# Residual rows added by accumulating loads, transposes and operand sums moved by a product, three operand fetches and one weight sum moved behind the last residual

## The chip, the cores and the metric

The kernel runs on one core of a Trainium2 chip, as one program. The metric is the device time of that program in microseconds. The core has a matrix engine (PE, with its weight loads shown as PEld), a vector engine (DVE), an activation engine (ACT), a general engine (POOL) that also issues DMAs, and a sync engine (SP) that only issues DMAs. Each engine takes its own instructions in the order that the build gave them, and waits on semaphores for the others. Sixteen DMA engines move all data.

## The reference

One layer of a hybrid decoder, on one sequence of 512 tokens with a model width of 2048, all in float32:

```python
h = rmsnorm(x, g_mix)
z = h @ w_in                         # conv B, C, V | attn Q, K, V | forget logits | two gates
...
merged = gc * conv_branch + ga * attn_branch
x = x + merged @ w_mix_out           # the mixing: this change
h = rmsnorm(x, g_mlp)
u = square(relu(h @ w_ff1))          # the MLP; its first group is fed by the mixing
x = x + u @ w_ff2
return rmsnorm(x, g_final)
```

The change concerns the line with `w_mix_out` and the hand-over to `w_ff1`.

## The kernel before

**Products.** Every large matrix product is done as a 2 by 2 block scheme with seven products in place of eight, named A11, A12, S1, S2, S3, S4 and A22. Each block operand is split into a high part and a low part (`split`, L102: the high part by a copy on ACT at L103, the low part by a subtraction on DVE at L104), and each product runs high by high, low by high and high by low, 48 matmuls for the blocks here. A class `Group` (from L190) does one set of 512 output columns: it loads the four quarters of the weights (`load`, on SP), splits them one after another into a pair of buffers of which there are two, runs the products into PSUM banks a, b, c, d, and hands the four result quarters to a `put`. After each product `run` calls the steps that a table `after` holds for it. The sums of weight quarters are subtractions on DVE (`sub`, L113).

**The mixing.** Four groups g = 0 to 3 of 512 columns each multiply the merged activations by `w_mix_out`. Groups 0 to 2 go A11, A12, S1, S3, S2, S4, A22 (`tail2`), group 3 goes A11, A12, S1, S2, S4, S3, A22 (`tail3`, L366). The quarters come out in the order (0,0), (1,1), (0,1), (1,0): row half, column half. Group 1's A11 runs between A11 and A12 of group 0.

For each result quarter (128 partitions by 2 by 256, in a tile of a ring of five called "o"), class `Mix` does this. `rows` (L1083) has loaded the matching rows of x into a tile xr, by POOL. `put` (L1088) adds xr on DVE, stores the sum to the DRAM tensor x1_d by POOL, and appends a **turn** to the list `waiting`. `turn` (L1098) squares the quarter on ACT for the norm, transposes it on PE (four transposes of 128 by 128, L1108), and copies the result with the norm's gain into the tiles F on ACT (L1117); in group 3 the turns of the upper half also write the last columns of A11 and A12 for the MLP (L1113 on ACT, L1114 on DVE). F's upper half is also stored to f_d.

When all four quarters of a group are turned, `first_of` and `sums` form the MLP's other operands S1, S2, S3, S4 from F on DVE; `give` splits each (the high part into one of two staging tiles, "staged") and stores it to h_d by POOL (`out`, L1125). For group 3 the operands are kept on chip.

**Where the steps stand.** Turns and splits are called from the `after` tables, so they stand at fixed places between products. ACT squares, PE transposes and staged splits are pinned: `tc.keep_in_program_order` puts an instruction behind whatever was traced on its engine just before it. What isn't pinned is ordered by a planner at build time, by priority and by its own estimate of when inputs are ready. A wait holds up everything behind it on its engine, and POOL waits for a DMA's landing before it issues one that depends on it.

**The hand-over.** The MLP's seven operands (`Q2`) take the SBUF places of the mixing's operands as those come free. `begin_part` (L1062) fetches what groups 0 to 2 stored: from f_d for A11 and A12, from h_d (1.5 MB each) for S1, S3, S2, S4, A22, all on POOL. `split_part` splits A11 and A12. The MLP's first group `g0` (L1283) runs A11 with the steps `first_sum` (L322: load the third quarter of `w_ff1` on SP, and subtract the first from it, pinned on DVE), `turn_waiting` (the last turn, (1,0)) and `first_of`. Then come A12, S1, S3 and so on; a third sum of weights is pinned on DVE too.

Of the kernel before, what the change touches and what calls it, by code (L numbers as in the profile page):

```python
# [8 lines left out]
F32 = mybir.dt.float32  # L9
# [36 lines left out]
def tile_hybrid_block(ctx: ExitStack, tc, x, g_mix, w_in, b_f, b_gate, conv_w, w_conv_out,  # L46
                      w_attn_out, w_mix_out, g_mlp, w_ff1, w_ff2, g_final, out):
    nc = tc.nc
# [21 lines left out]
    def otile(shape, name, dt=F32):  # L70
        return main.tile(shape, dt, tag="o", name=name, bufs=5)
# [40 lines left out]
    def sub(out, a, b):  # L112
        return nc.vector.tensor_tensor(out=out, in0=a, in1=b, op=ALU.subtract)  # L113

    def add(out, a, b):
        nc.vector.tensor_tensor(out=out, in0=a, in1=b, op=ALU.add)
# [73 lines left out]
    class Group:  # L190
# [128 lines left out]
            self.plus(s2, d)  # L319
            self.put(1, 0, s2)  # L320

        def first_sum(self):  # L322

            self.pinned = True
            X = self.X
            X[0, 1] = self.load(0, 1)
            tc.keep_in_program_order(sub(X[0, 0], X[0, 1], X[0, 0]))

        def tail2(self):

# [731 lines left out]
    def begin_part(n, k):  # L1062

        Q2[n] = pair(k, F32R, n).rearrange("p e (q s) -> p e q s", q=KT // 2)
        if n in SPLIT:
            nc.gpsimd.dma_start(out=Q2[n][:, :, :KT // 2 - 2].bitcast(F32), in_=h_d[:, SPLIT.index(n)])
        else:
            nc.gpsimd.dma_start(out=Q2[n][:, 1, :KT // 2 - 2].bitcast(F32), in_=f_d[:, int(n == "A12")])

    def split_part(n):  # L1070
        lo = Q2[n][:, 1, :KT // 2 - 2]
        split_in_order(lo.bitcast(F32), Q2[n][:, 0, :KT // 2 - 2], lo)

    class Mix:


        def __init__(self, g):
            self.g, self.last = g, g == 3
            self.F = [pm.tile([P, 2, 2, HS], F32, tag=f"f{i}", name="f") for i in range(2)]
            self.x = {}  # L1080
            self.rows(0, 0, pm.tile([P, 2, HS], F32, tag="xr", name="xr"))

        def rows(self, i, j, t):  # L1083
            c = self.g * S + j * HS
            nc.gpsimd.dma_start(out=t, in_=x[i * HS:(i + 1) * HS, c:c + HS].rearrange("(t p) c -> p t c", p=P))
            self.x[i, j] = t

        def put(self, i, j, v):  # L1088
            g = self.g
            c = g * S + j * HS  # L1090
            add(v, v, self.x.pop((i, j)))
            nc.gpsimd.dma_start(out=x1_d[2 * i:2 * i + 2, :, c:c + HS].rearrange("t p c -> p t c"), in_=v)
            waiting.append(lambda: self.turn(i, j, v))
            if (i, j) == (0, 0):
                self.rows(1, 1, otile([P, 2, HS], "xr"))
                self.rows(0, 1, pm.tile([P, 2, HS], F32, tag="xr", name="xr"))

        def turn(self, i, j, v):  # L1098
            g = self.g
            for t in range(2):  # L1100
                tc.keep_in_program_order(
                    square_part(v[:, t, :], ss2[:, 2 * i + t, 2 * g + j:2 * g + j + 1], bank(4, "junk")[:, :HS]))
# [77 lines left out]
    for g in range(4):  # L1180
        mix = mixes[g] = Mix(g)
        after = Steps()
        if g == 0:
            for n, n2 in zip(("A11", "A12", "S1", "S3", "S2"), ("S1", "S3", "S2", "S4", "A22")):
                after.add(n, quads3[n2])
        if g == 3:
            after.add("S1", mix.fourth, lambda: begin_part("A12", 4))
        late = g == 1
        for n in ("A12", "S3") if late else ("A11", "S1"):
            after.add(n, turn_waiting)  # L1190
        after.add("A22", turn_first)
        if before:
            after.add("A12" if late else "A11", before.first_of, before.sums)
            for n, part in (("A12", "S1"), ("S1", "S3"), ("S2", "A22")):
                after.add(n, lambda before=before, part=part: before.give(part))
        if g < 3:
            after.add("S2", mix.fourth)
        else:
            after.add("A12", lambda: begin_part("A11", 0))
            after.add("S2", lambda: begin_part("S1", 1), lambda: begin_part("S3", 3))  # L1200
            after.add("S4", lambda: split_part("A11"))
            after.add("S3", lambda: begin_part("S2", 5))
            after.add("A22", lambda: begin_part("S4", 6), lambda: begin_part("A22", 2), lambda: split_part("A12"))
        group = groups[g]
        group.after = after
        if g == 0:
            after.add("A11", group.first_sum)
        if g == 3:
            group.mid["A22"] = turn_first
        group.head(True, between=groups[1].first if g == 0 else lambda: None)  # L1210
        (group.tail2 if g < 3 else group.tail3)()
        before = mix
    def factors(common, r):

        ms = const.tile([P, NT], F32, name="ms")
# [61 lines left out]
    def ff1(g, banks):  # L1277
# [258 lines left out]
```

## Time and profile before

| | |
|---|---|
| median of 3 runs | 2448.05 us (2447.11 to 2450.04) |
| the profiled execution, whole | 2452.95 us |
| its span | 2451.2 us |
| mean granted clock of PE | 0.996 |
| mixing, first product to the end of the MLP's fourth | 1036.9 to 1238.3 us of the span |

A row of a window reads: start and end, length, then busy time and number of instructions of PE, PEld, DVE, ACT and POOL, the granted clock of PE as a share of full speed, the mean busy share of the DMA engines, and GB/s. A row of the timeline reads: start, duration, engine, line, operation, output and inputs, shapes, count; in brackets how long the engine was idle before it and what released it. A row of a tile's view reads: line, engine, operation, output and input, count, shortest, median and longest duration in ns, first and last start. A row of DMA issues ends in KB each and the median time from issue to landing. A row of the chain of waits reads: start, duration, what. Matmuls are pipelined and their ends are modelled, so the gap between two starts says more than a duration.

### The profile page before, as it was taken

What the parts mean: (1) busy time and instruction counts of PE and PEld (TensorE: products, weight loads), DVE (VectorE), ACT (ScalarE), POOL (GpSimd) and SP (SyncE); (2) the same over time, 40 slices, a digit from 0 to 9 for tenths busy, and PEclk for the clock granted to TensorE, in tenths of its full rate; (3) what the DMA queues carried; (4) which work ended last, traced back from release to release, by engine and by line L of the source; (5) the groups of instructions that cost most, each with busy time, mean ns of one, the idle gap of its engine ahead of it and who ended that gap; (6) DMA issues with size and microseconds to landing.
All of it is one profiled execution on the core that took longest, in us unless ns stands there. A gap on an engine that the chain in (4) does not pass through costs nothing.

```text
span 2451.2 us, 41539 instructions
## 1 busy us (share of the span) xinstructions
PE 2410.0 (98%) x17800; PEld 2266.2 (92%) x17800; DVE 2042.6 (83%) x1725; ACT 1203.0 (49%) x1233; POOL 280.0 (11%) x450
## 2 busy tenths in 40 slices
PE   8999999999999999999999999999999999999998
PEld 8999899999999999899899999999997888888886
DVE  6987777788888778898889898898978888889898
ACT  6443433345455444355656666666655333333334
POOL 0100000111121111112300000000011001100000
PEclk9999999999999999999999999999999999999999
DMA  7564444444656655757855655656587576655663
GB/s 250 181 187 147 154 135 143 142 154 167 216 170 214 213 189 189 237 162 252 306 183 186 228 189 199 236 182 228 194 304 271 168 248 227 236 190 183 245 223 103
DMA packets 287628, 491.97 MB, mean 201 GB/s; under 512 B 11900, under 2 KB 199412, under 8 KB 287060
## 3 DMA queue, kind: packets, MB, share of 16 engines
q1 hardware_dynamic: 237072, 283.20, 36.3%
q0 software_dynamic: 49504, 205.02, 22.5%
q8 instruction: 139, 2.28, 0.4%
q10 hardware_dynamic: 868, 1.10, 0.1%
q14 instruction: 45, 0.37, 0.0%
HBM read 378.65 MB, written 110.10 MB: 199 GB/s over the span
## 4 chain that ended last, share of the span: by engine, by line
PE 86%; DVE 5%; issue 4%; DMA 3%; POOL 1%; ACT 1%; DVEq 0%; SPq 0%; POOLq 0%; ACTq 0%
PE a L157 6%; PE a L153 6%; PE a L155 6%; PE a L175 5%; PE a L173 5%; PE a L172 5%; PE d L157 5%; PE d L153 5%; PE d L155 5%; PE c L153 4%; PE c L155 4%; PE c L157 4%; PE d L175 3%; PE d L173 3%; PE d L172 3%
## 5 line engine op out<-in xcount | busy, mean ns | idle before, releaser
L103 ACT ACTIVATE th<-x 128x2048 fp32r<-128x2048 f32 (+1 forms) x280 | 536.9, 1918 | 501.1 <-DVE x L113 169.3
L104 DVE TENSOR_TENSOR tl<-x,th 128x2048 fp32r<-128x2048 f32 (+1 forms) x280 | 639.5, 2289 | 166.3 <-ACT th L103 151.3
L113 DVE TENSOR_TENSOR x<-x,x 128x2048 f32<-128x2048 f32 (+1 forms) x160 | 366.3, 2289 | 28.5 <-DMA x<-in_w_in_dram 17.4
L103 ACT ACTIVATE th<-y 128x2048 fp32r<-128x2048 f32 (+1 forms) x109 | 185.4, 1702 | 273.8 <-PE a L173 138.8
L104 DVE TENSOR_TENSOR tl<-y,th 128x2048 fp32r<-128x2048 f32 (+1 forms) x109 | 219.1, 2014 | 29.1 <-ACT th L103 28.6
L172 PE MATMUL a<-th,us 128*128 128x512 f32 x512 | 199.4, 389 | 2.2 <-ACT th L103 2.2
L173 PE MATMUL a<-th,us 128*128 128x512 f32 x512 | 199.5, 390 | 0.0
L153 PE MATMUL c<-S,th 128*128 128x256 f32 x848 | 196.7, 278 | 0.0
L155 PE MATMUL c<-S,th 128*128 128x256 f32 x848 | 196.3, 277 | 0.0
L153 PE MATMUL a<-S,th 128*128 128x256 f32 x784 | 182.3, 278 | 0.0
L155 PE MATMUL a<-S,th 128*128 128x256 f32 x784 | 180.9, 277 | 0.0
L153 PEld LDWEIGHTS c<-S,th 128*128 128x128 f32 x848 | 159.4, 188 | 0.3
L155 PEld LDWEIGHTS c<-S,th 128*128 128x128 f32 x848 | 159.4, 188 | 0.0
L155 PEld LDWEIGHTS a<-S,th 128*128 128x128 f32 x784 | 147.4, 188 | 0.0
L153 PEld LDWEIGHTS a<-S,th 128*128 128x128 f32 x784 | 147.3, 188 | 0.0
L175 PE MATMUL a<-tl,us 128*128 128x512 f32 x512 | 137.0, 390 | 0.6 <-DVE tl L104 0.6
L155 PE MATMUL a<-A,th 128*128 128x256 f32 x544 | 126.0, 278 | 2.2 <-DVE A L1114 2.2
L153 PE MATMUL d<-S,th 128*128 128x256 f32 x544 | 128.0, 280 | 0.0
L155 PE MATMUL b<-A,th 128*128 128x256 f32 x544 | 126.4, 278 | 1.3 <-DVE A L104 1.3
L155 PE MATMUL d<-S,th 128*128 128x256 f32 x544 | 127.4, 279 | 0.0
L153 PE MATMUL b<-A,th 128*128 128x256 f32 x544 | 126.4, 278 | 0.0
L153 PE MATMUL a<-A,th 128*128 128x256 f32 x544 | 126.1, 278 | 0.0
(378 smaller groups left out, 6076.5 us busy)
## 6 DMA issues: line engine op xcount, KB each, us to landing
x<-in_w_in_dram SPq DMA_DIRECT2D x86, 1024.0 KB, 5.9
x<-in_w_ff_dram SPq DMA_DIRECT2D x64, 1024.0 KB, 8.5
y<-in_w_ff_dram SPq DMA_DIRECT2D x64, 1024.0 KB, 7.9
us<-s_d POOLq DMA_DIRECT2D x48, 1024.0 KB, 9.5
s_d<-rh POOLq DMA_DIRECT2D x32, 896.0 KB, 5.5
s_d<-r POOLq DMA_DIRECT2D x32, 896.0 KB, 5.9
x<-in_w_mix_out_dram SPq DMA_DIRECT2D x17, 1024.0 KB, 6.9
g_d<-o POOLq DMA_DIRECT2D x32, 256.0 KB, 2.8
```

Source lines behind the costliest of these rows:

```text
L103: a = nc.scalar.activation(out=hi, in_=src, func=AF.Copy, scale=one)
L104: b = nc.vector.tensor_tensor(out=lo, in0=src, in1=hi.bitcast(F32), op=ALU.subtract)
L113: return nc.vector.tensor_tensor(out=out, in0=a, in1=b, op=ALU.subtract)
L153: nc.tensor.matmul(o, hi[:, q, js], Sh, start=first and q == 0 and j == 0, stop=False, skip_group_check=True)
L155: nc.tensor.matmul(o, hi[:, q, js], Sl, start=False, stop=False, skip_group_check=True)
L157: nc.tensor.matmul(o, lo[:, q, js], Sh, start=False, stop=q == nq - 1, skip_group_check=True)
L172: nc.tensor.matmul(o, Sh, hi[:, q, :], start=begin and q == 0, stop=False, skip_group_check=True)
L173: nc.tensor.matmul(o, Sl, hi[:, q, :], start=False, stop=False, skip_group_check=True)
L175: nc.tensor.matmul(o, Sh, lo[:, q, :], start=False, stop=q == nq - 1, skip_group_check=True)
```

## The change

- `put` no longer adds x on DVE and stores. It issues one DMA on POOL that loads the rows of x **and adds them** to the quarter in SBUF (`accum_op=ALU.add`). The store to x1_d moves into `turn`. Group 3's two lower quarters (i = 1) keep the row load, DVE's addition and the store in `put`; their two row loads stay, the other 14 are gone.
- Turns are called one at a time, at new places: group 0's (0,0) after S3 instead of S1; in group 1 at A12, S1, S2, A22; in group 2 at A11, A12, S3, A22; in group 3 at A11, A12, S2, A22 (and the one in the middle of A22, as before). The turns at A22 stand where they stood.
- Sums and splits of the previous group follow one product later: in group 1 after S1, S3, S2 and S4, in groups 2 and 3 after A12, A12, S1 and S2.
- The fetch of S3 moves from after S2 to after S3 of group 3, those of S2, S4 and A22 into A11 of the MLP's first group, behind the last turn. The fetches from h_d are pinned on POOL.
- `first_sum` in the MLP's first group comes after the last turn and the fetches. Its subtraction is no longer pinned behind the previous instruction, but queued on DVE behind the last residual addition (`tc.issue_after`).

```diff
-        def first_sum(self):
+        def first_sum(self, pinned=True):
...
-            tc.keep_in_program_order(sub(X[0, 0], X[0, 1], X[0, 0]))
+            one = sub(X[0, 0], X[0, 1], X[0, 0])
+            if pinned:
+                tc.keep_in_program_order(one)
...
         if n in SPLIT:
-            nc.gpsimd.dma_start(out=Q2[n][:, :, :KT // 2 - 2].bitcast(F32), in_=h_d[:, SPLIT.index(n)])
+            tc.keep_in_program_order(
+                nc.gpsimd.dma_start(out=Q2[n][:, :, :KT // 2 - 2].bitcast(F32), in_=h_d[:, SPLIT.index(n)]))
...
-            self.rows(0, 0, pm.tile([P, 2, HS], F32, tag="xr", name="xr"))
+
+        def rows_of(self, i, j):
+            c = self.g * S + j * HS
+            return x[i * HS:(i + 1) * HS, c:c + HS].rearrange("(t p) c -> p t c", p=P)
...
+        def put(self, i, j, v):
+            if self.last and i == 1:
+                self.added = nc.vector.tensor_tensor(out=v, in0=v, in1=self.x.pop((i, j)), op=ALU.add)
+                self.store(i, j, v)
+            else:
+                nc.gpsimd.dma_start(out=v, in_=self.rows_of(i, j), accum_op=ALU.add)
+            waiting.append(lambda: self.turn(i, j, v))
+            if self.last and (i, j) == (0, 0):
+                self.rows(1, 1, pm.tile([P, 2, HS], F32, tag="xr", name="xr"))
...
-        def put(self, i, j, v):
-            g = self.g
-            c = g * S + j * HS
-            add(v, v, self.x.pop((i, j)))
             nc.gpsimd.dma_start(out=x1_d[2 * i:2 * i + 2, :, c:c + HS].rearrange("t p c -> p t c"), in_=v)
-            waiting.append(lambda: self.turn(i, j, v))
-            if (i, j) == (0, 0):
-                self.rows(1, 1, otile([P, 2, HS], "xr"))
-                self.rows(0, 1, pm.tile([P, 2, HS], F32, tag="xr", name="xr"))
 
         def turn(self, i, j, v):
             g = self.g
+            if not (self.last and i == 1):
+                self.store(i, j, v)
...
         if g == 3:
-            after.add("S1", mix.fourth, lambda: begin_part("A12", 4))
-        late = g == 1
-        for n in ("A12", "S3") if late else ("A11", "S1"):
-            after.add(n, turn_waiting)
-        after.add("A22", turn_first)
+            after.add("S1", mix.fourth)
+        for n in (("S3", "A22"), ("A12", "S1", "S2", "A22"), ("A11", "A12", "S3", "A22"), ("A11", "A12", "S2", "A22"))[g]:
+            after.add(n, turn_first)
         if before:
-            after.add("A12" if late else "A11", before.first_of, before.sums)
-            for n, part in (("A12", "S1"), ("S1", "S3"), ("S2", "A22")):
+            sums_at = ("S1", "S3", "S2", "S4") if g == 1 else ("A12", "A12", "S1", "S2")
+            after.add(sums_at[0], before.first_of, before.sums)
+            for n, part in zip(sums_at[1:], ("S1", "S3", "A22")):
                 after.add(n, lambda before=before, part=part: before.give(part))
-        if g < 3:
-            after.add("S2", mix.fourth)
-        else:
+        if g == 3:
             after.add("A12", lambda: begin_part("A11", 0))
-            after.add("S2", lambda: begin_part("S1", 1), lambda: begin_part("S3", 3))
+            after.add("S1", lambda: begin_part("A12", 4))
+            after.add("S2", lambda: begin_part("S1", 1))
             after.add("S4", lambda: split_part("A11"))
-            after.add("S3", lambda: begin_part("S2", 5))
-            after.add("A22", lambda: begin_part("S4", 6), lambda: begin_part("A22", 2), lambda: split_part("A12"))
+            after.add("S3", lambda: begin_part("S3", 3))
+            after.add("A22", lambda: split_part("A12"))
...
+    def begin_rest():
+        for n, k in (("S2", 5), ("S4", 6), ("A22", 2)):
+            begin_part(n, k)
+
+    def first_sum_after(ins):
+        with tc.issue_after(ins.ins):
+            g0.first_sum(pinned=False)
...
-    g0.after = Steps(A11=[g0.first_sum, turn_waiting, mix.first_of],
+    g0.after = Steps(A11=[turn_waiting, begin_rest, lambda: first_sum_after(mix.added), mix.first_of],
                      A12=[lambda: mix.out("S1", mix.s1), mix.sums, lambda: factors(common, turned)])
```

More of the change, by code (lines that the diff above doesn't have):

```diff
@@ L1080, in __init__, with store @@
             self.x = {}
-            self.rows(0, 0, pm.tile([P, 2, HS], F32, tag="xr", name="xr"))
+        def rows_of(self, i, j):
+            c = self.g * S + j * HS
+            return x[i * HS:(i + 1) * HS, c:c + HS].rearrange("(t p) c -> p t c", p=P)
         def rows(self, i, j, t):
-            c = self.g * S + j * HS
-            nc.gpsimd.dma_start(out=t, in_=x[i * HS:(i + 1) * HS, c:c + HS].rearrange("(t p) c -> p t c", p=P))
+            nc.gpsimd.dma_start(out=t, in_=self.rows_of(i, j))
             self.x[i, j] = t
         def put(self, i, j, v):
-            g = self.g
-            c = g * S + j * HS
-            add(v, v, self.x.pop((i, j)))
+            if self.last and i == 1:
[6 more added lines that the diff above has]
+                self.rows(1, 1, pm.tile([P, 2, HS], F32, tag="xr", name="xr"))
+        def store(self, i, j, v):
+            c = self.g * S + j * HS
             nc.gpsimd.dma_start(out=x1_d[2 * i:2 * i + 2, :, c:c + HS].rearrange("t p c -> p t c"), in_=v)
-            waiting.append(lambda: self.turn(i, j, v))
-            if (i, j) == (0, 0):
-                self.rows(1, 1, otile([P, 2, HS], "xr"))
-                self.rows(0, 1, pm.tile([P, 2, HS], F32, tag="xr", name="xr"))
         def turn(self, i, j, v):
             g = self.g
+            if not (self.last and i == 1):
+                self.store(i, j, v)
             for t in range(2):
```

## The prediction

> **What bounds the kernel now.** I read the page first, then the windows around the mixing, then each idle time of PE in them with its releaser, then the queues behind those releasers.
>
> ```profile
> span 2451.2 us, 41539 instructions
> PE 2410.0 (98%) x17800; PEld 2266.2 (92%) x17800; DVE 2042.6 (83%) x1725; ACT 1203.0 (49%) x1233; POOL 280.0 (11%) x450
> PE 86%; DVE 5%; issue 4%; DMA 3%; POOL 1%; ACT 1%; DVEq 0%; SPq 0%; POOLq 0%; ACTq 0%
> ```
>
> PE sets the time: 98% busy, and 86% of the chain that ended last. The change touches no product, so it can only gain PE's stalls in the mixing and at the hand-over to the MLP (first mixing product at 1036.9 us, the MLP's fourth product ends at 1238.28). Windows, with length, PE busy (instructions), granted clock, DMA share:
>
> ```profile
> 1036.90:1238.28 201.38, 190.28 (x1606) 187.78 (x1604) 173.02 (x150) 115.51 (x179) 49.81 (x78) 0.98 0.68 228
> 1238.28:1243.72 5.44, 5.44 (x51) 5.44 (x49) 4.69 (x3) 4.02 (x3) 0.00 (x0) 1.00 0.80 250
> ...
> 1100.17:1106.57 6.40, 5.72 (x52) 5.53 (x50) 6.24 (x7) 2.96 (x4) 3.53 (x7) 1.00 0.78 226
> 1106.57:1113.67 7.10, 5.72 (x48) 5.52 (x49) 1.41 (x3) 3.06 (x3) 2.32 (x5) 1.00 1.03 375
> 1113.67:1119.73 6.06, 5.82 (x48) 5.62 (x49) 5.69 (x4) 5.23 (x10) 0.71 (x1) 1.00 0.77 257
> 1119.73:1127.17 7.44, 6.92 (x63) 6.68 (x61) 7.44 (x8) 5.20 (x10) 1.63 (x3) 1.00 0.49 173
> 1173.59:1180.13 6.54, 5.60 (x50) 5.43 (x49) 6.54 (x8) 3.23 (x4) 0.91 (x2) 1.00 0.43 137
> 1180.51:1187.20 6.69, 5.84 (x51) 5.65 (x50) 6.69 (x8) 6.09 (x10) 4.44 (x8) 1.00 0.87 267
> 1192.64:1199.12 6.48, 5.61 (x50) 5.44 (x49) 4.40 (x6) 3.28 (x5) 2.88 (x5) 1.00 1.08 365
> ...
> 1205.56:1214.89 9.33, 7.18 (x51) 6.98 (x50) 6.34 (x6) 3.99 (x9) 5.06 (x7) 0.84 0.90 325
> 1214.89:1222.98 8.09, 6.79 (x56) 6.49 (x56) 7.18 (x9) 6.66 (x14) 1.41 (x1) 0.97 1.02 419
> 1222.98:1230.95 7.97, 5.91 (x52) 5.70 (x50) 5.93 (x13) 4.53 (x5) 0.56 (x1) 1.00 0.57 229
> 1230.95:1238.28 7.33, 7.33 (x50) 7.33 (x50) 7.26 (x4) 1.92 (x1) 0.00 (x0) 0.77 0.19 52
> ```
>
> The second row is an undisturbed product: 48 matmuls in 5.44 us, 0.1133 each. At that pace the first row's 1606 matmuls need 182.0 us of its 201.4: **19.4 us are lost**, and nothing here can gain more. The other rows hold 18.2 of them, each against 5.44 plus 0.35 for a turn's four transposes (0.35 is 1082.09 less 1081.74, further below the start of a turn and of the product after it). Group 1: S2 +0.96, S4 +1.66, A22 +0.62. Into group 2 (one product, three turns): +0.95. Group 3: S1 +1.10, S2 +1.25, S3 +1.04. Hand-over: A11 +3.89, turn and A12 +2.30, S1 +2.53, S3 +1.89. What ended PE's waits:
>
> ```profile
> 1113.67 0.38 PE L172 MATMUL d<-th,M 128*128 128x256 f32 x1 [1.38 <-ACT th L103]
> 1126.76 0.66 PE L1108 MATMUL ptr<-ident,o 128*128 128x128 f32 x4 [0.52 <-DVE o L116]
> 1180.13 0.63 PE L1108 MATMUL ptr<-ident,o 128*128 128x128 f32 x4 [0.94 <-DVE o L116]
> 1199.12 0.36 PE L172 MATMUL d<-th,M 128*128 128x256 f32 x1 [0.88 <-DVE o L116]
> 1211.25 0.39 PE L155 MATMUL a<-A,th 128*128 128x256 f32 x1 [2.15 <-DVE A L1114]
> 1230.95 0.36 PE L146 MATMUL d<-S,th 128*128 128x192 f32 x1 [2.06 <-ACT th L103]
> ```
>
> Two of them are turns waiting for a residual addition. The two waits above 2 us are followed by a lower clock (0.84 and 0.77 above), waits up to 1.38 are not (1.00): such a wait costs about 1.7 us more (A11's 3.89 less its 2.15; S3, with no wait inside its row, lost 1.89).
>
> The Trainium skill, "TensorE: Matmul & The Clock Gate", Part 1, lets the clock fall only after an idle window of some 3.4 us; by it no wait here would cost any clock, and the sum below would be 8.6 instead of 6.9 us. The trace disagrees at 2.15 and 2.06 us, so the measurement decides.
>
> **The change, part by part.**
>
> *Residual by accumulating load.* 14 of 16 additions leave DVE, at
>
> ```profile
> L1085 POOL DMA_DIRECT2D xr<-in_x_dram x16: 717/722/737, 1009.2 to 1183.7; - x16
> L116 DVE TENSOR_TENSOR o<-o,xr x16: 683/689/693, 1056.4 to 1211.8; 128x512 f32<-128x512 f32 x16
> ...
> DMA to landing us min/median/max: 3.2/3.9/10.1
> ```
>
> 0.689 us each: 9.6 us of DVE, off the path except where a turn waits for them. 16 plain row loads become 14 accumulating ones and two plain: POOL issues as many, bytes from x are the same. But the load now stands between sum and turn. Its time to land isn't in this trace. Low end: a plain load's 3.2 us. High end: it also reads and rewrites its tile, so a plain load plus a store (3.9 and a median of 3.0 below): 6.9, and about 10 where loads crowd. I take 5, nearer the load, whose packets it repeats.
>
> ```profile
> x_d<-o POOLq DMA_DIRECT2D x16, 256.0 KB, 3.0
> S<-h_d POOLq DMA_DIRECT2D x4, 1536.0 KB, 10.2
> ...
> 1074.98 0.68 DVE L116 TENSOR_TENSOR o<-a,o 128x512 f32<-128x512 f32 x1
> 1081.74 0.60 PE L1108 MATMUL ptr<-ident,o 128*128 128x128 f32 x4
> 1082.09 0.37 PE L172 MATMUL b<-th,M 128*128 128x256 f32 x1
> ...
> 1196.10 0.69 DVE L116 TENSOR_TENSOR o<-a,o 128x512 f32<-128x512 f32 x1
> 1202.02 0.60 PE L1108 MATMUL ptr<-ident,o 128*128 128x128 f32 x4
> ```
>
> Turns that don't move have this much room: group 0's (1,1), summed by 1075.66, turned at 1081.74: 6.1 us; group 3's (0,1), summed by 1196.79, turned at 1202.02 between A22's halves: 5.2 us. The load costs issue plus landing, 0.7 + 5: the first fits, the second is 0.5 late, and more, since the DMA share there is 1.08. I charge **2.5 us** for all late landings. The turns that move gain 5.44 us of room or more, and hide it.
>
> *Turns and sums a product later.* Each removes a turn's wait: +0.95 into group 2 and +1.10 in group 3, **2.0 us**. In group 1 the operands' splits come singly after S1, S3, S2, S4 instead of three after A12, so the two staging tiles need not be waited for:
>
> ```profile
> 1110.34 0.63 ACT L103 ACTIVATE staged<-f 128x512 fp32r<-128x512 f32 x1 [6.68 <-DMA h_d<-staged]
> ```
>
> ACT stood 6.7 us there, in order, with the split of A22's weights behind it (the 1.38 above). S4's 1.66 and A22's 0.62 go: **2.3 us**. S2's 0.96 and group 3's S2 and S3 (DVE busy throughout, or bank d still being read) stay. The mixing gains 4.3 us.
>
> *First sum behind the last residual.* Now it is pinned on DVE ahead of the last turns' operands:
>
> ```profile
> 1208.51 2.29 DVE L113 TENSOR_TENSOR x<-x,x 128x2048 f32<-128x2048 f32 x1 [6.33 <-DMA x<-in_w_ff_dram]
> 1210.72 0.48 DVE L1114 SCALAR_TENSOR_TENSOR A<-ptr,cols,A 128x256 fp32r<-128x256 f32 x1
> ...
> 1220.00 0.68 DVE L116 TENSOR_TENSOR s<-f 128x512 f32<-128x512 f32 x1
> 1226.61 2.29 DVE L113 TENSOR_TENSOR x<-x,x 128x2048 f32<-128x2048 f32 x1
> ...
> 1190.88 17.54 DMA x<-in_w_ff_dram
> ```
>
> DVE stood 6.33 us for weights that took 17.5 us to land (at 1208.42), with A11's last columns queued behind. After the change L1114 and A12's split run in that hole, so A11 loses nothing. Next is late what follows the weights: first sum 2.29, one split of that size, then as now from 1220.00 to the third sum's end at 1228.90 (8.9), then its split on ACT until PE starts at 1230.95 (2.05): 1208.4 + 15.5 = 1223.9 for S3. PE would get there at 1205.56 + 3 x 5.44 + 0.35 = 1222.2. So S3 starts at 1223.9 instead of 1230.95, with no wait long enough for the clock: 7.05 + 1.89 = **8.9 us**. If DVE's hole is filled otherwise (A11's operand still late), all but the clock of S3 stays lost.
>
> The two gains do not add whole: with PE 4.3 us earlier the weights land earlier only in part, as the DMA engines are full from 1192 on. I let half come through, so 2.15 is given back, and the clock's 1.7 too, since S3 then waits over 2 us: 3.85.
>
> *Three fetches behind the last residual.* Today S2, S4 and A22 leave between 1209 and 1213, since POOL stands before them:
>
> ```profile
> 1195.12 0.71 POOL L1066 DMA_DIRECT2D S<-h_d  x1 [9.57 <-DMA h_d<-s]
> 1208.01 0.71 POOL L1066 DMA_DIRECT2D S<-h_d  x1 [10.01 <-DMA h_d<-f]
> ```
>
> The new place is behind (1,0)'s sum, addition and store: 1205.6 + 2 x 0.69 + 0.73 = 1207.7, one POOL issue apart. On POOL they pass nothing but that store; S3's fetch now comes behind the (0,1) load, so that load isn't queued after its 1.5 MB. S2's product begins at 1238.28 today, some 7 to 9 us earlier then: 1229; its fetch lands at 1218, the third by 1238 even at 10.2 us each, for a product that starts two later, at 1240. Zero, hidden by A11 to S4; without that cover each us late is a us of PE.
>
> Sum: 4.3 + 8.9 − 3.85 − 2.5 = **6.9 us faster**. The profiled execution took 2452.95 us (span 2451.2 plus 1.75); it would be 2446.1. It lies 4.9 above the median of the runs, 2448.05, so I forecast **2441**.
>
> **The rivals.**
>
> *Accumulating loads land late (slower).* A turn is pinned in PE's order, so a late load stops PE. For: loads took up to 10.1 us here. Against: the median is 3.9. At 8 us (plus 0.7) the two turns computed wait 2.6 and 3.5; with half of the 14 waiting 2 us each, 14, and one lowered clock, 1.7, against 9.35 (the sum without the 2.5): 6 us slower, **2454**. It decides from about 7 us of issue plus landing (9.35/7 = 1.3 above the 5.65 that the two have on average).
>
> *POOL stands ahead of the last accumulating load.* S1's fetch is pinned and waits for its operand's last store (the 9.57 above); sums come a product later, so this ends at 1195 + 5.4 = 1200.6, and group 3's (0,1) load queues behind: landing at 1200.6 + 0.7 + 3.9 = 1205.2, a wait of 3.2 and 1.7 of clock, 4.9; behind the 1.5 MB themselves (10.2) at 1211, 9 and 1.7. Between them 7.5, in place of the 2.5: 1.9 us faster, **2446**. Against: the planner may put the load first.
>
> The Trainium skill, "DMA: Bandwidth & Descriptors", Anatomy of one DMA, speaks for it: a DMA's wait is done by the issuing sequencer. Its rules add that whoever touches an accumulating DMA's bytes must wait for its semaphore, so each x1 store now also stands on POOL. The 9.57 agrees with the first; no run here shows the second yet.
>
> *All of it comes through*: the weights land 4.3 us earlier and no load is late: 4.3 + 8.9 less about 1 for what stays at S3: **2436**.
>
> *It doesn't do what it says*: the planner orders turns, loads and splits so that the same waits return elsewhere: **2448**.
>
> **How the numbers follow.** Forecast (2438 to 2444.5) 0.40; all 0.14; POOL 0.14; no effect 0.07; late landings 0.25. Range: 0.1 off each end, **2434 to 2455**; the forecast's own range stands in brackets. A measurement here tells about 0.2%, 4.9 us, from no change. Faster by more: 0.14 + 0.9 of 0.40 = 0.50. Slower by more (over 2453): most of the late landings, 0.23. Between: 0.27.
>
> **What would show it.** Right: no PE wait on DVE before L1108; no wait for staging tiles in group 1; A11 near 5.5 us; S3 of the MLP's first group starting about 7 to 9 us earlier, after a wait under 4 us; landing of the accumulating loads near 5. Wrong: PE waiting at a transpose for a DMA, above all in the middle of group 3's A22; POOL idle for tens of us before x1 stores; A11 still waiting for L1114.

## The result and the profile after

The changed kernel takes 2484.79 us (median of 5 runs, 2481.62 to 2486.4) against 2447.89 for the kernel before on the same chip: **1.0149 times** as long, 95% interval 1.0134 to 1.0163. The forecast was 2441, the range 2434 to 2455.

The page of the changed kernel, its first lines and the chain's shares by engine:

```profile
span 2482.7 us, 41525 instructions
PE 2420.5 (97%) x17800; PEld 2275.0 (92%) x17800; DVE 2034.6 (82%) x1711; ACT 1202.8 (48%) x1233; POOL 287.6 (12%) x450
PE 83%; issue 6%; DMA 4%; DVE 4%; POOL 1%; ACT 1%; POOLq 0%; SPq 0%; DVEq 0%; ACTq 0%
```

DVE did 8 us less work, POOL 8 us more, and the span grew by 31.5. (The medians differ by 36.9: the profiled execution of the kernel before took 2452.95 us, 5 above its median.) Two windows split the stretch: the mixing from its first product to the start of the MLP's A11, and the hand-over from there to the end of S3. Before:

```profile
1036.91:1205.56 168.65, 163.07 (x1406) 161.27 (x1404) 146.30 (x121) 98.41 (x152) 42.78 (x69) 1.00 0.68 221
1205.56:1238.28 32.72, 27.21 (x204) 26.51 (x202) 26.71 (x29) 17.10 (x28) 7.03 (x9) 0.90 0.69 264
```

After, with two products of the mixing that follow a wait of PE:

```profile
1035.99:1240.28 204.29, 175.15 (x1405) 171.85 (x1404) 138.95 (x108) 99.00 (x151) 52.49 (x72) 0.95 0.67 196
1240.28:1269.73 29.45, 25.81 (x202) 25.33 (x201) 26.11 (x29) 16.02 (x29) 4.84 (x6) 0.92 0.52 199
...
1111.59:1118.88 7.29, 7.29 (x48) 7.29 (x49) 2.98 (x2) 2.92 (x3) 1.27 (x3) 0.77 0.79 255
1129.87:1136.68 6.81, 6.81 (x50) 6.81 (x49) 4.50 (x3) 3.75 (x9) 3.37 (x4) 0.80 0.49 118
```

The mixing lost 35.6 us, the hand-over gained 3.3. PE's idle time in the mixing rose from 5.6 us (168.65 less 163.07) to 29.1; the other 12.1 us are the same matmuls taking longer, at a mean clock of 0.95 instead of 1.00. PE's waits above 2 us, and the shortest of its four for a DMA, from the changed kernel's timeline:

```profile
1082.47 0.63 PE L1119 MATMUL ptr<-ident,o 128*128 128x128 f32 x4 [1.28 <-DMA o<-in_x_dram]
1111.59 0.38 PE L172 MATMUL c<-th,M 128*128 128x256 f32 x1 [2.44 <-DVE o L116]
1129.13 1.08 PE L1119 MATMUL ptr<-ident,o 128*128 128x128 f32 x4 [4.44 <-DMA o<-in_x_dram]
1179.29 1.09 PE L1119 MATMUL ptr<-ident,o 128*128 128x128 f32 x4 [5.57 <-DMA o<-in_x_dram]
1217.18 0.38 PE L172 MATMUL d<-th,M 128*128 128x256 f32 x1 [2.36 <-ACT th L103]
1227.03 0.36 PE L172 MATMUL d<-th,M 128*128 128x256 f32 x1 [2.40 <-DVE o L116]
1238.48 1.09 PE L1119 MATMUL ptr<-ident,o 128*128 128x128 f32 x4 [4.22 <-DMA o<-in_x_dram]
1262.63 0.53 PE L146 MATMUL d<-S,th 128*128 128x192 f32 x1 [2.95 <-ACT th L103]
```

The four waits for a DMA are the four turns that did not move: (1,1) of groups 0 to 2, and (0,1) of group 3. (In the trace this last one stands ahead of A22's last matmul; in the kernel before it stood between A22's halves.) The view of waits over 1036 to 1270 us (engine, line waited at, releaser: total, times, longest) shows who else stands:

```profile
POOL x_d L1105 <- DMA o<-in_x_dram: 53.3, 13, 8.6
ACT junk L460 <- DMA o<-in_x_dram: 48.2, 13, 6.4
DVE tl L104 <- ACT th L103: 40.5, 16, 8.6
...
PE ptr L1119 <- DMA o<-in_x_dram: 15.5, 4, 5.6
ACT staged L103 <- DMA h_d<-staged: 14.6, 4, 4.4
```

The same loads hold POOL at the x1 store, ACT at the pinned squares and PE at the transposes; DVE then waits for ACT's weight splits, 40.5 us where the kernel before had 12.4 from its first mixing product to the end of S3. Rows of POOL and DVE in the changed kernel's timeline, for group 0's last two quarters and group 1's first:

```profile
1080.50 0.68 DVE L116 TENSOR_TENSOR o<-a,o 128x512 f32<-128x512 f32 x1
...
1082.62 0.75 POOL L1105 DMA_DIRECT2D x_d<-o  x1 [6.16 <-DMA o<-in_x_dram]
1083.36 1.24 POOL L1098 DMA_DIRECT2D o<-in_x_dram  x1
1088.18 0.75 POOL L1105 DMA_DIRECT2D x_d<-o  x1 [3.57 <-DMA o<-in_x_dram]
1088.92 1.24 POOL L1098 DMA_DIRECT2D o<-in_x_dram  x1
1093.46 0.75 POOL L1105 DMA_DIRECT2D x_d<-o  x1 [3.30 <-DMA o<-in_x_dram]
1094.20 1.26 POOL L1098 DMA_DIRECT2D o<-in_x_dram  x1
```

Each load is followed by its own store, which stands until it has landed, so the loads leave 5.3 to 5.6 us apart: the sum that ended at 1081.18 is loaded onto only at 1083.36, and that load lands 4.3 us later (a landing is counted from the start of the issue, so the 1.24 us of issue are part of it). The loads that PE waited for took longer. That of group 3's (0,1) left right behind the fetch of S1 and took 11.04 us, by POOL's timeline and the chain of waits; the view of line L1098 gives the spread of all 14:

```profile
1226.59 0.72 POOL L1069 DMA_DIRECT2D S<-h_d  x1
1227.30 1.26 POOL L1098 DMA_DIRECT2D o<-in_x_dram  x1
...
1227.30 11.04 DMA o<-in_x_dram
...
DMA to landing us min/median/max: 4.2/4.3/11.0
```

In the order of the groups, the four that PE waited for took 7.1, 5.2, 7.3 and 11.0 us.

### The profile page after: what moved, and what is told of

It reads as the page before. It is cut to its first block, busy times and chain, and to the rows that moved or that the text cites. A ratio compares the mean times of both kernels' runs of the same rounds, so it can differ in the third digit from the quotient of the medians.

```text
span 2482.7 us, 41525 instructions
## 1 busy us (share of the span) xinstructions
PE 2420.5 (97%) x17800; PEld 2275.0 (92%) x17800; DVE 2034.6 (82%) x1711; ACT 1202.8 (48%) x1233; POOL 287.6 (12%) x450
## 4 chain that ended last, share of the span: by engine, by line
PE 83%; issue 6%; DMA 4%; DVE 4%; POOL 1%; ACT 1%; POOLq 0%; SPq 0%; DVEq 0%; ACTq 0%
PE a L157 6%; PE a L153 6%; PE a L155 6%; PE a L173 5%; PE a L172 5%; PE a L175 5%; PE d L153 5%; PE d L155 5%; PE d L157 5%; PE c L153 4%; PE c L155 4%; PE c L157 3%; PE d L172 3%; PE d L173 3%; PE d L175 3%
```

## The experiments

All of them in one table. Ratios are to the kernel before, run on the same chip; its medians lay between 2447.9 and 2452.6 us on the different chips, so ratios compare better than times. "Mixing" and "hand-over" are the two windows above, in us, from one profiled execution of each run.

| run | us | ratio, 95% interval | mixing | hand-over |
|---|---|---|---|---|
| before | 2447.89 | 1 | 168.7 | 32.7 |
| changed | 2484.79 | 1.0149 (1.0134, 1.0163) | 204.3 | 29.5 |
| e1 all additions on DVE | 2454.15 | 1.0018 (1.0007, 1.0029) | 177.4 | 26.9 |
| e2 hand-over alone | 2450.46 | 0.9997 (0.9987, 1.0006) | 167.5 | 33.9 |
| e3 loads alone | 2476.68 | 1.0108 (1.0086, 1.0130) | 204.1 | 24.0 |
| e4 stores a turn later | 2484.51 | 1.0129 (1.0110, 1.0147) | 205.8 | 30.7 |
| e5 no squares | 2480.53 | 1.0116 (1.0101, 1.0131) | 198.6 | 27.8 |
| e6 four quarters on DVE | 2471.60 | 1.0080 (1.0063, 1.0097) | 193.3 | 26.9 |
| e7 stores pinned later | 2477.47 | 1.0100 (1.0085, 1.0115) | 197.2 | 31.2 |
| e8 e6 without squares | 2460.12 | 1.0041 (1.0025, 1.0057) | 184.3 | 27.2 |
| e9 turns later still | 2462.48 | 1.0049 (1.0034, 1.0065) | 189.5 | 26.6 |
| e10 late fetches | **2444.01** | **0.9973 (0.9962, 0.9984)** | 168.4 | 26.6 |
| e11 late fetches alone | 2447.91 | 0.9987 (0.9978, 0.9996) | 168.7 | 27.6 |
| e12 e8, stores pinned later | 2456.27 | 1.0024 (1.0015, 1.0034) | 176.7 | 27.2 |
| e13 places, groups 0 and 1 | 2448.01 | 0.9993 (0.9984, 1.0003) | 171.0 | 26.7 |
| e14 places, groups 2 and 3 | 2452.76 | 1.0014 (1.0004, 1.0023) | 178.0 | 26.9 |
| e15 e14, splits spread by one | 2458.67 | 1.0036 (1.0022, 1.0050) | 209.3 together | |
| e16 e14, splits spread by two | 2455.45 | 1.0011 (1.0001, 1.0020) | 207.7 together | |

### Loads, places, hand-over: one at a time

*e1.* The changed kernel with plain row loads and DVE's additions again.

```diff
...
-                nc.gpsimd.dma_start(out=v, in_=self.rows_of(i, j), accum_op=ALU.add)
+            self.added = nc.vector.tensor_tensor(out=v, in0=v, in1=self.x.pop((i, j)), op=ALU.add)
+            self.store(i, j, v)
...
```

> Theory L (the load): the changed kernel lost its 31 us because an accumulating load stands between a quarter's sum and its turn, and PE's transposes (15.5 us of waits) and ACT's squares (48.2 us) stand for it. Then plain row loads and DVE's additions in all the new places are near the kernel before, 2443 to 2450 us. Theory P (the places): turns and sums a product later crowd the splits, the two staging tiles and the reuse of F; then this stays slow, 2465 us or more.

*e2.* The kernel before with the hand-over's edits alone.

```diff
...
-            after.add("S2", lambda: begin_part("S1", 1), lambda: begin_part("S3", 3))
+            after.add("S2", lambda: begin_part("S1", 1))
...
-    g0.after = Steps(A11=[g0.first_sum, turn_waiting, mix.first_of],
+    g0.after = Steps(A11=[turn_waiting, begin_rest, lambda: first_sum_after(mix.added), mix.first_of],
```

> The kernel before with the hand-over's edits alone (three fetches behind the last residual, fetches pinned, first sum queued behind the last addition). My forecast's term for it was 8.9 us: 2439 us. The changed kernel's own rows (29.5 us for the hand-over against 32.7) say 3 us: 2445. If the pinned fetches hold POOL, nothing or slower, 2448 or more.

*e3.* The kernel before with the changed kernel's `put`, `store` and `turn`, at the old places and with the old hand-over.

```diff
...
-            add(v, v, self.x.pop((i, j)))
...
+                nc.gpsimd.dma_start(out=v, in_=self.rows_of(i, j), accum_op=ALU.add)
...
```

> The kernel before with the accumulating loads alone, turns and sums in the old places. Theory L: worse than the changed kernel, since the turns have less room: 14 turns with up to 5.5 us each, 2490 us or more. Theory P: near the kernel before, 2448 to 2458.

**e1** took the mixing from 204.3 to 177.4: the loads cost 26.9 us, and the places, which were forecast to gain, cost the 8.8 that remain. **e3**, with the loads at the old places, has a mixing as long as the changed kernel's (204.1), so there the loads cost 35.4 us; they stop PE at nine turns, 28.1 us in all, the longest 9.0. That the loads cost more there was right, but the 2490 us expected were not reached: without loads the new places cost 8.8 us, and with them they take PE's waits off by about as much as they cost elsewhere. **e2** gained nothing. In its timeline A11 no longer waits, but what follows does:

```profile
1209.95 2.29 DVE L113 TENSOR_TENSOR x<-x,x 128x2048 f32<-128x2048 f32 x1 [6.00 <-DMA x<-in_w_ff_dram]
...
1210.41 0.36 PE L146 MATMUL b<-A,th 128*128 128x192 f32 x1 [1.58 <-ACT A L103]
1214.30 0.58 PE L153 MATMUL c<-S,th 128*128 128x256 f32 x1 [3.40 <-ACT th L103]
```

and its chain of waits says what for:

```profile
1187.56 22.38 DMA x<-in_w_ff_dram
```

The weights took 22.4 us to land instead of 17.5, and the first sum began at 1209.95 instead of 1208.51, although PE reached A11 2.9 us earlier (1202.69). Rows of POOL in e2 show what else was under way:

```profile
1191.85 0.72 POOL L1069 DMA_DIRECT2D S<-h_d  x1 [2.29 <-DMA h_d<-s]
1196.59 0.72 POOL L1069 DMA_DIRECT2D S<-h_d  x1 [1.08 <-DMA h_d<-f]
```

In the program S3's fetch comes later than before, but in time it left at 1196.59 instead of 1208.01, since POOL waited less for the stores ahead of it. So both fetches of 1.5 MB fell into the landing of these weights, where before S3's left only 0.4 us ahead of its end.

### What the loads hold up

*e4* and *e7* let the x1 store wait for the next turn; e7 also pins loads and stores, so that on POOL the next load goes first.

```diff
-            if not (self.last and i == 1):
-                self.store(i, j, v)
+            while stores:
+                stores.pop(0)()
+            if not (self.last and i == 1):
+                stores.append(lambda: self.store(i, j, v))
...
```

> The changed kernel with each x1 store issued at the next turn, so that POOL need not stand for the load that it has just issued. If POOL's 53.3 us of waits before x1 stores are what makes the loads late, PE's waits for them (15.5 us) fall to a third and the time to 2460 to 2472 us. If the load's own issue and landing (1.24 + 4.3 us) is the matter, 2480 to 2486.

e4 told nothing: unpinned, the store was again planned right behind its load, and POOL stood 53.2 us at it as before. In e7 POOL stands 7.7 us there, and ACT 31.8 us at the squares instead of 48.2; PE's waits for loads rose all the same, from 15.5 to 18.4 us.

> The changed kernel with loads and x1 stores pinned on POOL in the order load, then the store of the load before: no load stands behind the store of its direct predecessor. Theory Q: issue of the loads follows the sums at once (1.2 us apart instead of 5.3), the third and fourth load of a group land 4 to 8 us earlier, ACT's standing halves, and a third to a half of the 31 us comes back: 2465 to 2475. Theories T and A: the loads that PE waits for are the first after a pause on POOL, nothing is queued ahead of them but operand stores; 2478 to 2486, PE's waits for a load 12 us or more.

*e5* takes ACT's wait away by leaving the squares out, so that the MLP's norm works with a constant in place of its statistics.

```diff
...
-            for t in range(2):
-                tc.keep_in_program_order(
-                    square_part(v[:, t, :], ss2[:, 2 * i + t, 2 * g + j:2 * g + j + 1], bank(4, "junk")[:, :HS]))
```

> The changed kernel without the 32 squares of the residual rows on ACT (the statistics of the second norm are left out, so that later scaling uses a constant); loads, stores, turns and all else as in the changed kernel. Theory A (ACT stands for the loads at the pinned squares, 48.2 us at 13 places in the changed kernel, and weight splits, snaps and so the sums behind it come late): most of that standing goes, sums come earlier, the PE waits for a load at the four unmoved turns fall from 15.5 us to under 8, and the time to 2460 to 2470. Theory T (the load simply doesn't fit between sum and turn at the four unmoved turns, and the lowered clock behind each wait does the rest: 15.5 + 4 x 1.7 = 22 of the 31 us): ACT was only standing early, PE's waits stay at 12 to 16 us, 2478 to 2486. Theory Q (POOL: each load stands behind the store of its predecessor): as under T.

*e6* takes the loads away where PE waits for them.

```diff
...
-            if self.last and i == 1:
+            if self.by_dve(i, j):
...
+        def by_dve(self, i, j):
+            return (i, j) == (1, 1) or self.last and (i, j) != (0, 0)
```

> The changed kernel with the additions of the four quarters whose turn did not move ((1,1) of groups 0 to 2, (0,1) of group 3) back on DVE behind plain loads and stored at once; ten accumulating loads remain, for quarters whose turns moved a product later. Theory T: PE's waits at transposes for a load are gone, and with them the clock drops: 22 us or more of the 31 come back, 2452 to 2462, about as with all additions on DVE (2454). Theory A: ACT still stands for ten loads at the squares (some 30 us), splits stay late: 2465 to 2475. Theory Q: the remaining loads still stand behind stores, but nothing waits for them but ACT: 2460 to 2475.

None of the three theories was enough. e7 gave back 7.1 us of mixing, e5 5.7, e6 11.0. (e5 is the least sure: its interval, 1.0101 to 1.0131, overlaps that of e4, which made no difference.) In e6 PE's four long waits for a load are gone, but others came up, in its timeline:

```profile
1132.05 0.66 PE L1124 MATMUL ptr<-ident,o 128*128 128x128 f32 x4 [1.30 <-DMA o<-in_x_dram]
1188.20 0.58 PE L172 MATMUL c<-th,M 128*128 128x256 f32 x1 [1.98 <-ACT th L103]
1222.57 0.55 PE L172 MATMUL d<-th,M 128*128 128x256 f32 x1 [4.35 <-DVE o L116]
```

with ACT still standing 32.4 us at nine places for the ten other loads. So the edits were joined. *e8* is e6 with e5's, *e12* is e8 with e7's.

> The changed kernel with both edits at once: the four quarters whose turn did not move are added on DVE, and the 32 squares on ACT are left out (the statistics of the second norm). Mixing in the changed kernel 204.3 us, with the four quarters alone 193.3, with all additions on DVE 177.4. Theory T+A (what the four quarters leave is ACT standing at the squares, 32.4 us there, ahead of weight splits): mixing 176 to 182, time 2452 to 2459. Theory Q (what is left is POOL: operand stores queued behind loads and x1 stores, so that ACT and DVE wait for the staging tiles): mixing 188 to 193, 2464 to 2470, with ACT waiting at staged and f for stores.

> The kernel with the four unmoved quarters added on DVE and the squares left out (mixing 184.3 us), and x1 stores of the accumulated quarters pinned on POOL behind the next load. With all additions on DVE mixing took 177.4. Theory Q (the 6.9 us left are POOL's: operand stores behind loads and x1 stores, ACT waiting 18.5 us for the staging tiles): ACT's wait for staging falls under 10 us, mixing 176 to 181, time 2452 to 2457. Rival (the loads' own order costs it, POOL waits as long for other sums): 182 to 188, 2458 to 2464.

Step by step the mixing goes 204.3, 193.3 (four loads away), 184.3 (squares away), 176.7 (stores behind the next load): 11.0, 9.0 and 7.6 us, the last of which reaches what additions on DVE give (177.4). The ratios go the same way, 1.0149, 1.0080, 1.0041, 1.0024, though the intervals of the last two overlap. So all three holds cost time; the squares are worth more once the four loads are gone (9.0 instead of 5.7), the stores about the same (7.6 instead of 7.1). The split is not clean: e12 still has PE standing 6.72 us at one turn and ACT 14.5 us for staging tiles (under 10 was expected), and leaving the squares out also saves ACT their own work, which e1 still does.

*e9* keeps all but one of these loads and turns (1,1) of groups 0 to 2 a product later, with the turns, the sums and S1's fetch behind it; group 3's (0,1) is added on DVE.

```diff
-        for n in (("S3", "A22"), ("A12", "S1", "S2", "A22"), ("A11", "A12", "S3", "A22"), ("A11", "A12", "S2", "A22"))[g]:
+        for n in (("S3",), ("A12", "A12", "S1", "S2"), ("A11", "A12", "S1", "S2"), ("A11", "A12", "S1", "S2", "A22"))[g]:
...
```

> The changed kernel with the turns of (1,1) in groups 0 to 2 a product later (with them (0,0) of the later groups, and the sums behind), by accumulating loads still; (0,1) of group 3, which can't move, is added on DVE. Theory T (room between sum and turn): no PE wait for a load over 1 us, mixing 190 to 196, 2464 to 2473, as where the four are added on DVE (193.3; 2471.6). Theory A: the squares are pinned at the turns and move with them, so ACT stands less as well: mixing 180 to 190, 2455 to 2465. If neither, and operands that come a product later hold PE or DVE instead: 2473 to 2486.

PE's longest wait for a load fell to 0.49 us, and the mixing to 189.5, below e6's 193.3: with a product of room the load itself no longer stops PE. The other holds stay, and PE now waits 9.62 us once at group 3's A22 for DVE's sum.

### The hand-over

*e10* is e2 with the fetches of S1 and S3 behind the last residual too; *e11* has only the five late fetches (pinned on POOL as in e2), and the first sum pinned where it was.

```diff
-            after.add("S2", lambda: begin_part("S1", 1))
...
-            after.add("S3", lambda: begin_part("S3", 3))
...
-        for n, k in (("S2", 5), ("S4", 6), ("A22", 2)):
+        for n, k in (("S1", 1), ("S3", 3), ("S2", 5), ("S4", 6), ("A22", 2)):
```

> The kernel before with the hand-over's edits, and the fetches of S1 and S3 behind the last residual too (five there instead of three). With the three alone the MLP's weights landed after 22.4 us at 1209.9 and held DVE's first sum (hand-over 33.9 us). Theory W (the fetches crowd the weights: DMA share 1.00 to 1.06 from 1185 to 1220): weights land in 15 to 19 us, the first sum starts 3 to 6 us earlier, hand-over 27 to 31, 2442 to 2447. Rival R (the crowding comes from the mixing's own weights and stores): landing stays over 20 us, 2448 to 2452; or S1's 1.5 MB come too late and PE waits for them at S1: 2452 to 2458.

> The kernel before with one edit: all five fetches of split operands (S1, S3, S2, S4, A22) behind the last residual; the first sum keeps its pinned place ahead of the last turns' operands. Tells whether the time gained with the hand-over's edits and late fetches (2444.0; hand-over 26.6 us against 32.7) is the fetches' alone. Theory W (the weights' landing sets the hand-over): they land near 1203 to 1206, the pinned first sum is done before A11 needs its last columns, hand-over 26 to 29, 2442 to 2447. Rival P (the pin costs: DVE still stands for the weights ahead of A11's columns): A11 waits 1 to 2 us and the clock falls, hand-over 29 to 33, 2447 to 2451.

e10 is the fastest version; only e10 and e11 have a whole interval below 1. The two windows of e10:

```profile
1035.05:1203.44 168.39, 163.95 (x1405) 161.99 (x1404) 148.44 (x127) 99.19 (x153) 43.48 (x70) 1.00 0.68 221
1203.44:1230.08 26.64, 23.71 (x203) 23.11 (x201) 24.50 (x22) 15.22 (x26) 15.12 (x8) 1.00 0.83 322
```

The hand-over is 6.1 us shorter and its clock whole. The first sum, in e10's timeline, has no wait any more:

```profile
1204.62 2.28 DVE L113 TENSOR_TENSOR x<-x,x 128x2048 f32<-128x2048 f32 x1
```

In e11's chain of waits the weights land in 13.5 us:

```profile
1190.09 13.46 DMA x<-in_w_ff_dram
```

5.2 of the 6.1 us are there without the first sum's new place. The run times say less (0.13% for e11, 0.27% for e10, with intervals that overlap), so how much the first sum's place adds stays open. e2 and e10 differ only in the fetches of S1 and S3. With both of these 1.5 MB fetches leaving early in their landing the weights took 22.4 us (e2, where the three late fetches also left in its last 3.1 us), with S1's alone 17.5 (before), and with none 13.5 (e11). So the landing of the weights set the hand-over, and the fetches were what crowded it.

### Where the places cost

On e10's base: *e13* has the new places of turns and sums in groups 0 and 1 alone, *e14* in groups 2 and 3.

```diff
...
+        if g in (0, 1):
+            for n in (("S3", "A22"), ("A12", "S1", "S2", "A22"), ("A11", "A12", "S3", "A22"), ("A11", "A12", "S2", "A22"))[g]:
+                after.add(n, turn_first)
...
+                sums_at = ("S1", "S3", "S2", "S4") if g == 1 else ("A12", "A12", "S1", "S2")
```

> The kernel before with the hand-over's edits and late fetches (mixing 168.4 us, hand-over 26.6), and the changed kernel's places of turns and sums in groups 0 and 1 alone; all additions on DVE. Tells where the places, which with all additions on DVE made the mixing 177.4 us long, cost it. Theory G3 (the places cost in groups 2 and 3, where ACT waits for the staging tiles ahead of weight splits, products of 9.4 and 10.5 us there): groups 0 and 1 gain or lose nothing, mixing 166 to 170, 2441 to 2446. Rival (the sums of group 1 come a product later and make its own unmoved turn wait, 1.65 us seen): 170 to 173, 2446 to 2450.

> As the last, with the new places in groups 2 and 3 alone. Theory G3: mixing 174 to 178, PE waiting for DVE or ACT at products of group 3 (S1, S4, S3), 2450 to 2454. Rival (the cost lies in group 1): 167 to 171, 2442 to 2447.

Groups 0 and 1 lose 2.6 us (168.4 to 171.0): PE waits 1.76 and 2.38 us at two of group 1's turns for DVE's residual additions. Groups 2 and 3 lose 9.6, all of it in group 3: up to the start of S2 e14 is 1.2 us ahead of e10, then S2 takes 10.4 us instead of 6.7, S3 10.6 instead of 6.5, and A22 with its turns 8.7 instead of 6.4. In group 3 of e14 ACT stands for a staging tile again (5.70 us): S1's split now follows A12 together with those of S2 and S4, three splits for two tiles, as in group 1 of the kernel before. *e15* and *e16* take S1's split away from there.

```diff
-                sums_at = ("S1", "S3", "S2", "S4") if g == 1 else ("A12", "A12", "S1", "S2")
+                sums_at = ("A12", "S3", "S2", "S4") if g == 2 else ("A12", "S2", "S4", "S3")
```

That is e16; e15 has `("A12", "S1", "S3", "S2")` and `("A12", "S1", "S2", "S4")`.

> As with the new places in groups 2 and 3 alone (mixing 178.0), but the sums' operands leave singly: S2 and S4 with the sums at A12, S1, S3 and A22 one product later each, not S1 at A12 too. Theory B (three splits after one product want a third staging tile where there are two; ACT stood 14.8 us for them in the mixing there, 5.70 ahead of a weight split in group 3): ACT's wait for staging under 7 us, mixing 168 to 172, 2442 to 2448. Rival (the turns or the sums themselves are too late, whatever the splits): 175 to 179, 2449 to 2453.

> As with the new places in groups 2 and 3 alone (mixing 178.0), with the splits of S1, S3 and A22 two products behind those of S2 and S4 and one apart, so that the next weight split on ACT goes ahead of S1's. (Only one product behind, S1's split was still queued ahead of that weight split, stood 6.72 us for a staging tile, and nothing was won.) Theory B (two staging tiles, three splits): no staging wait ahead of a weight split, mixing 168 to 172, 2442 to 2448. Rival (turns and sums late as such): 175 to 179, 2449 to 2456.

The staging theory fell. In e15 the wait stayed (6.72 us); in e16 it no longer stands ahead of the weight split, and still nothing was won. (In both, 12 and 14 matmuls of A11 ran ahead of the last half product, so the two windows are given together: 209.3 and 207.7, against 204.9 in e14.) What all three share, in e16's timeline:

```profile
1178.83 0.68 DVE L116 TENSOR_TENSOR o<-b,o 128x512 f32<-128x512 f32 x1
1179.43 0.68 DVE L116 TENSOR_TENSOR s<-f 128x512 f32<-128x512 f32 x1
1180.03 0.68 DVE L1094 TENSOR_TENSOR o<-o,xr 128x512 f32<-128x512 f32 x1
1180.63 0.68 DVE L113 TENSOR_TENSOR f<-f 128x512 f32<-128x512 f32 x1
1181.23 2.28 DVE L104 TENSOR_TENSOR tl<-x,th 128x2048 fp32r<-128x2048 f32 x1
...
1183.57 1.20 PE L175 MATMUL a<-tl,M 128*128 128x256 f32 x8 [2.82 <-DVE tl L104]
```

The operand sums (the second and the fourth row) now fall into the stretch in which DVE adds up A12's quarter, ahead of the split that S2 needs. PE's wait there is 2.75, 2.82 and 2.82 us in e14, e15 and e16, and 0.85 in e10. How much of it the sums make is not shown: the two take 1.2 us, in e10 DVE does 1.8 us of other operand work at the same place, and in e14 PE also comes 1.3 us earlier, because no turn stands there any more. All three versions wait once more, 4.3 to 5.1 us, at A22 or at the MLP's A11. No run took either wait away by itself, so the cause of group 3's loss stays open beyond these two waits.

## Why the prediction was wrong, step by step

**The bound** held: nothing gained more than a part of the 19.4 us; e10's two windows come to 195.0 against 201.4.

**"I charge 2.5 us for all late landings"** is the step that failed most: the loads cost 26.9. Four things were wrong in it:
- *The landing.* The 5 us taken fit the median, 4.3 (the 0.7 of issue was counted twice). But the four loads that PE waited for took 7.1, 5.2, 7.3 and 11.0 us. In groups 0 and 3 PE reached the turn 6.2 and 8.0 us after the sum, and a load of 5.7 would have been hidden there.
- *The room.* "Turns that don't move have this much room" was read from groups 0 and 3. Group 1's row says otherwise, in the kernel before:

```profile
1115.86 0.68 DVE L116 TENSOR_TENSOR o<-a,o 128x512 f32<-128x512 f32 x1
...
1119.73 0.60 PE L1108 MATMUL ptr<-ident,o 128*128 128x128 f32 x4
```

  Sum done at 1116.54, turn at 1119.73: 3.2 us for a load taken at 5.7. And the sums came later in the changed kernel, behind ACT's delayed splits: PE reached the turns of groups 1 and 2 only 1.5 and 2.4 us after them, where group 2 had 7.1 before.
- *The consumers.* "The turns that move gain 5.44 us of room or more, and hide it" counted PE alone. The squares, pinned on ACT, stand for the same load in front of the weight splits; e5 and e8 put 5.7 and 9.0 us on that.
- *The queue.* "POOL issues as many" is true (450 instructions in both), but each load is now followed by a store that must see it land, so POOL hands the loads out one landing apart. e7 and e12 put 7.1 and 7.6 us on that. The Trainium skill, "DMA: Bandwidth & Descriptors", Anatomy of one DMA, was cited ahead for exactly this, that the issuing sequencer does a DMA's wait; the 53.3 us of POOL at L1105 agree. The rival built on it looked only at one load, group 3's (0,1). For that load it was right: it left 0.7 us behind S1's fetch, landed late, and PE waited 4.2 us.

**"The mixing gains 4.3 us"** by later turns and sums: they lose 8.8 (e1); tried alone, 9.6 in groups 2 and 3 (e14) and 2.6 in groups 0 and 1 (e13). In group 1 the wait of 6.68 us for staging tiles fell to 3.99 (e13), but two turns there then waited for DVE. That the new table gives groups 2 and 3 three splits after A12 stood in the diff and was passed over. Spreading them gained nothing, though (e15, e16); what makes the later sums and turns dear in group 3 is only in part known.

**"8.9 us" at the hand-over, and "Zero" for the three fetches.** The chain behind the weights was the right one, but the landing of 17.5 was held fixed. With the edits alone it is 22.4, since a fetch that stands later in the program left earlier, and they bring nothing (e2). In the changed kernel the 3.3 us are probably none of their doing: PE reaches A11 at 1240.28, and the weights have landed at 1226.2. In e3 they have landed too, and with no such edit it gains 8.7. With the landing short, e10 gained 6.1, not far from the 8.9 or from the 5.05 that were left of it after the 3.85.

Together, in the windows: places -8.8, loads -26.9, hand-over +3.3, 32.4 us slower, where the forecast had +4.3, -2.5 and +5.05.

**The clock** went as said in this trace: PE's 2.44 and 4.44 us are followed by products at 0.77 and 0.80, 1.9 and 1.4 us longer than 5.44. By the rule of the Trainium skill, "TensorE: Matmul & The Clock Gate", Part 1, that a fall wants an idle window of some 3.4 us, the first would have cost none; the trace disagrees again. Other runs show that 2 us is no limit either (last section).

**The rival** of late landings had the side right (2454). That its first price, PE's waits, came out near (14 us; measured 15.5) is luck: it took seven waits of 2 us, and there were four of 1.3 to 5.6. It had no term for ACT and POOL, and took the places and the hand-over as gains.

## What to carry to other kernels

Before an addition is moved from a vector engine into a DMA, list everything that touches the tile behind it, on every engine and in the issuing queue, and read the room of each in every iteration: the shortest one decides, and pinned work on a side engine passes the delay on to the main one. Where the DMA engines are full, the order of transfers by need can be worth more than fewer vector instructions: putting five fetches behind the weights needed first was the only edit here that made the kernel faster. A step moved by one product in four places is four changes, and what it lands on differs in each.

## What the runs showed of the hardware

An accumulating load is dearer to issue than a plain one. From the changed kernel's groups by line, and its DMA issues:

```profile
L1098 POOL DMA_DIRECT2D o<-in_x_dram x14 | 17.3, 1238 | 37.7 <-DVE o L116 37.3 <-issue 0.3
...
o<-in_x_dram POOLq DMA_DIRECT2D x14, 256.0 KB, 4.3
```

1.24 us of POOL each against 0.72 for the plain load of as many bytes, while the landing, counted from the start of the issue, is hardly longer: a median of 4.3 against 3.9.

The length of PE's wait alone did not tell whether its clock falls. Behind a wait of 1.90 us in e8 and one of 3.02 us in e12:

```profile
1239.34:1244.84 5.50, 5.50 (x34) 5.50 (x35) 5.43 (x3) 2.00 (x3) 0.00 (x0) 0.69 0.01 3
...
1207.28:1212.78 5.50, 5.50 (x47) 5.42 (x48) 4.15 (x5) 1.13 (x3) 1.89 (x4) 1.00 0.94 275
```

The granted clock is 0.69 behind the shorter wait and 1.00 behind the longer one. So the prediction's 1.7 us per wait above 2 us holds for the cases that it was read from, and for the changed kernel's, but is no rule.
